# Six plain column blocks instead of four in a ConvGLU mixer, and a later rank for the sums of squares of its norm

## The chip, the core and the metric

The kernel runs on one NeuronCore of a Trainium2 chip. The metric is the device time of one execution in microseconds; before and after are compared by the median of several runs. The engines are named as the profile names them: PE (TensorE matmul), PEld (its weight loads), DVE (VectorE), ACT (ScalarE), POOL (GpSimd), SP (SyncE, which issues the DMAs here).

## What is computed

An encoder trunk of two layers over 512 positions of width 1024, all in float32. Cut to what matters here:

```python
for l in range(DEPTH):                                   # DEPTH = 2
    ...                                                  # attention: two head groups, then
    x = x + jnp.einsum('bsm,md->bsd', y, w_out[l])       # the output projection
    h = rmsnorm(x, g_ffn[l])                             # x * rsqrt(mean(x*x) + EPS) * g
    gate, val = jnp.split(jnp.einsum('bsd,df->bsf', h, w_up[l]), 2, axis=-1)
    gate = centred_dwconv(gate, conv_w[l], conv_b[l])    # width 3
    x = x + jnp.einsum('bsf,fd->bsd', jax.nn.silu(gate) * val, w_down[l])
```

D_FF is 2816: 22 blocks f of 128 columns, each with a gate product and a value product of depth 1024.

## The kernel before

**Layout and products.** The residual stream x lies in SBUF as eight tiles x_0 to x_7 of 128 features by 512 positions. A float32 product is made of three fast ones: each operand is split into a rounded high part and the rest (h and l; wh and wl for weights), and a product is high by high, high by low, low by high, all summed in one PSUM bank (`mm3`). A weight unit is loaded by SP into `wr`, rounded by ACT (a CAST to `wh`), and the rest is taken by DVE (`wl<-wr,wh`). There are two `wr` buffers and three each of `wh` and `wl`.

**The norm of the mixer (class `Norm`, name nf).** The mixer's products run on g*x without the factor r = rsqrt(mean square); r is applied later. `add(k)` makes nf_h (ACT) and nf_l (DVE) of tile k as soon as the last output projection has added to x_k. `squares` makes x_k*x_k on ACT (`nf_q`, the first straight into `nf_sum`) and adds it into `nf_sum` on DVE. `rms` then takes the sum over features with eight PE records (`nf_ss`), DVE makes `nf_v`, POOL `nf_r` by a power, and `rb_track` spreads r over the partitions with PE (`rps`) and copies it on ACT (`rb`).

**The plain path (`up_step`).** One product of 24 matmuls of 512 columns for the gate of block f (`up_f_0`), one for its value (`up_f_1`). The gate's bank is freed when DVE has made `gp = bank * rb`; then come the conv (`cv`, ACT and two DVE instructions), SiLU (ACT), `cv * rb` on POOL, the multiplication by the value's bank on DVE, and the split for the down projection (`act_out`). Five PSUM banks serve these products.

**The halved pairs (`pair_step`, `up_pair`).** Two blocks f and f+1 together as a 2 by 2 block product with seven half products instead of eight: 84 matmuls of 256 columns for the gates, 84 for the values. They need "forms" of h (sums and differences of halves, `ha` to `fc`, made once per layer by `mixer_forms` as soon as rb is there), four sums of weights on DVE per pair and half (`ws`), and DVE puts the results together (`du`, `gp`, `dp`). The last half product of a pair must wait for the first `du`.

**Order.** `mixer_order` gives, for the first part (blocks 0 to 5), four plain blocks and the pair 4; after that pairs 6, 8, 10, ... stand between the steps of the down projection `dn`. `PLAIN` is the number of plain blocks. The order of every engine is fixed when the program is built: a planner (`Machine.run`, line 258 is its issuing line, so all trace rows carry L258) takes the operation that can start first, and among those that can start within a short hold the one with the smallest rank. The ranks stand in `RK`: `xl` 8 for the last additions to x and the nf_h and nf_l after them, `w` 2, 45 or 30 for weight units (36 `wf` when one is ready ahead in the mixer), `hf` 22 for the forms, `nsq` for the squares and their sums. Engines then run their queues in that order; a waiting instruction holds everything behind it on its engine.

Of the kernel before, what the change touches and what calls it, by code (L numbers as in the profile page):

```python
# [26 lines left out]
EPS = 1e-6  # L27
NEG = -1e30
FF_PARTS = ((0, 6), (6, 12), (12, 18), (18, 22))
PLAIN = 4  # L30
CHUNKS = ("akv", "aq0", "aq1", "bv0", "bk1", "bk0", "bq0", "bq1", "bv1")
CW = 256
RP = 4
# [11 lines left out]


RK = {"w": (2, 45, 30), "qkb": (55, 18), "x": 33, "xl": 8, "a": 2, "b": 18, "evac": 49, "qka": 60, "kv": 45,
      "bn": 2, "nsq": 6, "av": -4, "bv": 4, "ch": 50, "add": 42, "sec": 1, "nxs": 42, "fin": 42, "sum": 25,
      "hf": 22, "wf": 36}


# [250 lines left out]
def kernel(  # L302
# [72 lines left out]
    def mixer_order():  # L375

        ups = [[(f, 1) for f in range(f0, min(f1, PLAIN))] + [(f, 2) for f in range(max(f0, PLAIN), f1, 2)]
               for f0, f1 in FF_PARTS]
        for f, n in ups[0]:
            yield "up", 0, f, n  # L380
        for pi in range(len(FF_PARTS)):
            after = ups[pi + 1] if pi + 1 < len(FF_PARTS) else []
            at = {NK * i // len(after): u for i, u in enumerate(after)}
            for d in range(NK):
                if d in at:
                    yield ("up", pi + 1, *at[d])
                yield "dn", pi, d, 0
# [277 lines left out]
    def layer(l, norm):  # L665
# [862 lines left out]
        def ffn():  # L1528
            steps = list(mixer_order())
            b_st["rb_left"] = PLAIN + 1  # L1530
            mix["forms"] = 14
# [149 lines left out]
```

## Time and profile before

| | |
|---|---|
| median of 3 runs | 1184.47 us (1183.8 to 1187.16) |
| the profiled execution: time, span | 1185.19 us, 1183.1 us |
| busy in the span: PE, DVE, ACT, POOL | 98%, 83%, 56%, 17% |
| mean granted TensorE clock | 0.993 |
| first mixer product of layer 0, of layer 1 | starts 236.20 us, 823.03 us |
| first halved pair of layer 0, of layer 1 | starts 288.48 us, 875.38 us |

The span runs from the first to the last instruction of the core. Matmuls are pipelined, so a row's duration (0.39 us for 512 columns) is longer than the step to the next row's start (0.2275 us): what a matmul costs in a stream is read from starts, and where PE is late is seen where the step between two starts is longer than that. Where a row has a pair of brackets, the engine stood idle for that time before it, and the name behind the arrow ended it.

### The profile page before, as it was taken

Reading aid. Unit: us, or ns where it says so; the run is one execution under the profiler, and the core shown is the slowest. Engines: PE = TensorE matmul, PEld = TensorE weight load, DVE = VectorE, ACT = ScalarE, POOL = GpSimd, SP = SyncE. Lnnn points to the kernel's source line nnn. Section 1 sums busy time; section 2 is a strip of 40 time slices with the busy share of each in tenths; the row PEclk is TensorE's granted clock in tenths of the full one; section 3 lists DMA queues with packets and bytes.
Section 4 is the critical chain, followed back from the end, with each engine's and each line's share of the span. In section 5 each row is a group of like instructions: output and inputs, shape, how many; then the busy total and the mean of one; then the engine's idle time right before and its main releaser. Section 6 shows DMA issues by size and latency. Waiting matters only on the chain.

```text
span 1183.1 us, 20177 instructions
## 1 busy us (share of the span) xinstructions
PE 1163.1 (98%) x7796; PEld 1053.0 (89%) x7796; DVE 981.9 (83%) x1797; ACT 663.2 (56%) x1187; POOL 202.3 (17%) x254
## 2 busy tenths in 40 slices
PE   9999999999999999999999989999999999999998
PEld 7999888978999999999889989888789999999997
DVE  6988899779998888887659888898799988888863
ACT  6779766455564454444537876665555544544441
POOL 2433721010100000000042556110111000000000
PEclk9999999989999999999999999999899999999999
DMA  6221111123223322332332121111232223233323
GB/s 233 66 72 55 54 55 36 54 72 107 68 99 112 111 99 99 112 125 71 107 118 73 37 71 37 55 54 54 71 124 61 96 88 112 98 112 103 121 81 116
DMA packets 33343, 103.12 MB, mean 87 GB/s; under 512 B 3936, under 2 KB 4192, under 8 KB 33248
## 3 DMA queue, kind: packets, MB, share of 16 engines
q1 hardware_dynamic: 33248, 101.84, 26.0%
q8 instruction: 61, 1.00, 0.4%
q14 instruction: 34, 0.28, 0.1%
HBM read 99.73 MB, written 2.10 MB: 86 GB/s over the span
## 4 chain that ended last, share of the span: by engine, by line
PE 79%; DVE 13%; ACT 5%; issue 2%; POOL 0%; DMA 0%; SPq 0%; DVEq 0%; ACTq 0%
PE up L258 32%; PE dn L258 20%; PE wo L258 6%; PE pj_bk L258 3%; PE pj_bv L258 2%; PE pj_akq L258 2%; PE pj_bq L258 2%; DVE wl L258 2%; PE yb L258 2%; PE sc_b L258 2%; PE pt_a L258 1%; PE pv_a L258 1%; PE sc_a L258 1%; PE wt_b L258 1%; ACT so_a L258 1%
## 5 line engine op out<-in xcount | busy, mean ns | idle before, releaser
L258 ACT CAST wh<-wr 128x1024 fp32r<-128x1024 f32 (+2 forms) x200 | 177.2, 887 | 158.9 <-PE up L258 41.3
L258 DVE TENSOR_TENSOR wl<-wr,wh 128x1024 fp32r<-128x1024 f32 (+2 forms) x193 | 196.7, 1020 | 62.9 <-ACT wh L258 62.7
L258 ACT CAST wh<-ws 128x1024 fp32r<-128x1024 f32 x72 | 75.4, 1048 | 109.2 <-DVE ws L258 46.1
L258 PE MATMUL up<-fc,wh 128*128 128x256 f32 x576 | 106.4, 285 | 1.8 <-DVE du L258 1.8
L258 PE MATMUL up<-fa,wh 128*128 128x256 f32 x576 | 107.0, 283 | 0.0
L258 PE MATMUL up<-fb,wh 128*128 128x256 f32 x576 | 105.6, 284 | 0.0
L258 PEld LDWEIGHTS up<-fc,wh 128*128 128x128 f32 x576 | 89.4, 191 | 2.6 <-ACT cv L258 2.1
L258 PEld LDWEIGHTS up<-fb,wh 128*128 128x128 f32 x576 | 89.8, 192 | 0.4 <-ACT dp L258 0.2
L258 PEld LDWEIGHTS up<-fa,wh 128*128 128x128 f32 x576 | 89.8, 192 | 0.1
L258 DVE TENSOR_TENSOR wl<-ws,wh 128x1024 fp32r<-128x1024 f32 x72 | 89.5, 1245 | 0.4 <-ACT wh L258 0.2
L258 PE MATMUL dn<-act,wh 128*128 128x512 f32 x288 | 88.9, 390 | 0.0
L258 PE MATMUL up<-fa,wl 128*128 128x256 f32 x288 | 81.7, 284 | 0.0
L258 PE MATMUL up<-fb,wl 128*128 128x256 f32 x288 | 81.5, 283 | 0.0
L258 PE MATMUL up<-fc,wl 128*128 128x256 f32 x288 | 81.4, 283 | 0.0
L258 PE MATMUL dn<-acth,wh 128*128 128x512 f32 x208 | 81.0, 389 | 0.0
L258 PE MATMUL dn<-actl,wh 128*128 128x512 f32 x208 | 81.0, 389 | 0.0
L258 PE MATMUL dn<-acth,wl 128*128 128x512 f32 x208 | 80.9, 389 | 0.0
L258 POOL TENSOR_TENSOR du<-du 128x256 f32<-128x256 f32 x12 | 8.9, 742 | 395.9 <-DVE du L258 395.9
L258 DVE TENSOR_TENSOR x<-x,dn 128x512 f32<-128x512 f32 x64 | 43.7, 682 | 32.8 <-PE dn L258 32.8
L258 DVE SCALAR_TENSOR_TENSOR cv<-gp,cols,cv 128x512 f32<-128x512 f32 x88 | 63.9, 745 | 0.0
L258 PEld LDWEIGHTS dn<-act,wh 128*128 128x128 f32 x288 | 53.3, 188 | 10.4
L258 ACT ACTIVATE e_b<-sc_b,mx_b,rqb 128x512 f32<-128x512 f32 x64 | 49.1, 776 | 14.6 <-DVE mx_b L258 14.6
(269 smaller groups left out, 3452.4 us busy)
## 6 DMA issues: line engine op xcount, KB each, us to landing
wr<-w_up SPq DMA_DIRECT2D x88, 512.0 KB, 4.5
wr<-w_down SPq DMA_DIRECT2D x48, 384.0 KB, 3.1
wr<-w_in SPq DMA_DIRECT2D x28, 512.0 KB, 3.5
wr<-w_out SPq DMA_DIRECT2D x16, 512.0 KB, 3.4
wr<-w_down SPq DMA_DIRECT2D x16, 256.0 KB, 2.6
x<-xT SPq DMA_DIRECT2D x8, 256.0 KB, 5.5
prob_f<-w_first SPq DMA_DIRECT2D x8, 256.0 KB, 5.6
wr<-w_first SPq DMA_DIRECT2D x4, 512.0 KB, 3.6
```

Of the source, the lines that this page charges most:

```text
L258: getattr(self.raw[op.eng], op.name)(*op.args, **op.kw)
```

## The change

Two numbers. `PLAIN` goes from 4 to 6: in each layer blocks 4 and 5 are made by two plain steps instead of one halved pair, so the whole first part is plain and the pair 6 is the first. And the rank `nsq` goes from 6 to 44: the squares of the mixer's norm and their sums give way to everything with a smaller rank, among it the nf_h and nf_l (8) and weight units that are needed (2).

```diff
-PLAIN = 4
+PLAIN = 6
...
-      "bn": 2, "nsq": 6, "av": -4, "bv": 4, "ch": 50, "add": 42, "sec": 1, "nxs": 42, "fin": 42, "sum": 25,
+      "bn": 2, "nsq": 44, "av": -4, "bv": 4, "ch": 50, "add": 42, "sec": 1, "nxs": 42, "fin": 42, "sum": 25,
```

The planner makes new orders of it. DVE's queue in layer 0 where the output projection ends and the mixer begins, before (x are the last additions, nf_l the low parts that PE waits for, nf_sum the sums of squares, wl weight units):

```order
L258 TENSOR_TENSOR x_71<-x_71,wo_2_1_5_3062 128x256
L258 SCALAR_TENSOR_TENSOR nf_l_3082<-x_68,cols,nf_h_3064 128x512
L258 TENSOR_TENSOR wl_3068<-wr_2873,wh_3052 128x1024
L258 SCALAR_TENSOR_TENSOR nf_l_3094<-x_69,cols,nf_h_3078 128x512
L258 TENSOR_TENSOR nf_sum<-nf_sum,nf_q_3098 128x512
L258 SCALAR_TENSOR_TENSOR nf_l_3119<-x_70,cols,nf_h_3085 128x512
L258 TENSOR_TENSOR nf_sum<-nf_sum,nf_q_3121 128x512
L258 SCALAR_TENSOR_TENSOR nf_l_3128<-x_71,cols,nf_h_3091 128x512
L258 TENSOR_TENSOR nf_sum<-nf_sum,nf_q_3130 128x512
L258 TENSOR_TENSOR x_72<-x_72,wo_2_1_6_3074 128x256
L258 TENSOR_TENSOR nf_sum<-nf_sum,nf_q_3137 128x512
L258 TENSOR_TENSOR x_73<-x_73,wo_2_1_7_3087 128x256
```

The same place after:

```order
L258 TENSOR_TENSOR x_71<-x_71,wo_2_1_5_3063 128x256
L258 TENSOR_TENSOR wl_3060<-wr_2873,wh_3052 128x1024
L258 SCALAR_TENSOR_TENSOR nf_l_3076<-x_68,cols,nf_h_3065 128x512
L258 SCALAR_TENSOR_TENSOR nf_l_3087<-x_69,cols,nf_h_3070 128x512
L258 SCALAR_TENSOR_TENSOR nf_l_3097<-x_70,cols,nf_h_3078 128x512
L258 SCALAR_TENSOR_TENSOR nf_l_3107<-x_71,cols,nf_h_3082 128x512
L258 TENSOR_TENSOR x_72<-x_72,wo_2_1_6_3074 128x256
L258 TENSOR_TENSOR x_73<-x_73,wo_2_1_7_3091 128x256
L258 TENSOR_TENSOR wl_3114<-wr_2957,wh_3101 128x1024
L258 SCALAR_TENSOR_TENSOR nf_l_3132<-x_72,cols,nf_h_3128 128x512
L258 SCALAR_TENSOR_TENSOR nf_l_3139<-x_73,cols,nf_h_3130 128x512
L258 TENSOR_TENSOR nf_sum<-nf_sum,nf_q_3055 128x512
```

All seven additions into nf_sum now stand behind the last nf_l; one more weight unit (wl_3114) has come ahead of the last two nf_l. Layer 1 has the same order.

PE's queue at the same place, before (nf_ss is the sum over features, rps the spreading of r):

```order
L258 MATMUL up_0_0_3100<-nf_h_3148,wl_2942 128x512
L258 MATMUL nf_ss<-unit,nf_sum 128x1 x4
L258 MATMUL up_0_1_3166<-nf_h_3023,wh_3052 128x512
L258 MATMUL up_0_1_3166<-nf_l_3030,wh_3052 128x512
L258 MATMUL up_0_1_3166<-nf_h_3023,wl_3068 128x512
```

And after:

```order
L258 MATMUL up_0_1_3152<-nf_h_3130,wl_3060 128x512
L258 MATMUL nf_ss<-unit,nf_sum 128x1 x4
L258 MATMUL up_1_0_3200<-nf_h_3023,wh_3101 128x512
L258 MATMUL up_1_0_3200<-nf_l_3030,wh_3101 128x512
L258 MATMUL up_1_0_3200<-nf_h_3023,wl_3114 128x512
```

nf_ss has moved from behind the first product to behind the second; rps follows nine matmuls after nf_ss in both.

DVE's queue at the first `du` of the first halved pair of layer 0, before (pair 4; actl is the low part of a finished block, wl units are weights of this pair):

```order
L258 TENSOR_TENSOR wl_3598<-wr_1_3345,wh_3592 128x512
L258 TENSOR_TENSOR actl_1_3572<-cv_1_3280,acth_1_3571 128x512
L258 SCALAR_TENSOR_TENSOR cv_2_3386<-gp_2_3385,cols,cv_2_3386 128x512
L258 TENSOR_TENSOR wl_3618<-wr_0_3349,wh_3611 128x1024
L258 TENSOR_TENSOR du_4_0_3529<-dp_4_0_3528,up_4_0_3_3610 128x256
```

And after (pair 6):

```order
L258 TENSOR_TENSOR actl_4_3736<-cv_4_3566,acth_4_3735 128x512
L258 SCALAR_TENSOR_TENSOR cv_5_3650<-gp_5_3649,cols,cv_5_3650 128x512
L258 TENSOR_TENSOR wl_3758<-wr_1_3524,wh_3752 128x512
L258 TENSOR_TENSOR du_6_0_3692<-dp_6_0_3691,up_6_0_3_3771 128x256
L258 TENSOR_TENSOR wl_3778<-wr_0_3531,wh_3772 128x1024
```

The 1024-wide weight unit that stood ahead of the first du now stands behind it. Apart from blocks 4 and 5 and the places of nf_ss and rps, PE's order of products is the same in both programs, in both layers.

## Rows read from the trace of the kernel before

**Rows 1.** The page: busy time of the engines with share of the span, and the chain of work that ended last, by engine.

```profile
PE 1163.1 (98%) x7796; PEld 1053.0 (89%) x7796; DVE 981.9 (83%) x1797; ACT 663.2 (56%) x1187; POOL 202.3 (17%) x254
...
PE 79%; DVE 13%; ACT 5%; issue 2%; POOL 0%; DMA 0%; SPq 0%; DVEq 0%; ACTq 0%
```

**Rows 2.** Busy time by stretch at the start of the mixer of layer 0 (236 us on) and layer 1 (823 us on). Columns: stretch, its length, busy us and instructions of PE, PEld, DVE, ACT, POOL, then granted clock, DMA share, GB/s.

```profile
236.20:241.30 5.10, 4.49 (x19) 2.90 (x18) 5.10 (x8) 4.62 (x8) 0.00 (x0) 1.00 0.30 103
241.30:244.70 3.40, 1.97 (x6) 0.74 (x5) 3.40 (x7) 2.38 (x4) 0.00 (x0) 1.00 0.00 0
244.70:251.60 6.90, 6.74 (x20) 5.67 (x21) 3.15 (x5) 1.05 (x1) 2.08 (x5) 0.51 0.43 143
...
828.40:831.80 3.40, 1.79 (x6) 0.78 (x6) 3.40 (x8) 2.38 (x4) 0.00 (x0) 1.00 0.00 0
831.80:838.70 6.90, 6.90 (x22) 5.80 (x23) 2.88 (x4) 1.05 (x1) 2.08 (x5) 0.51 0.48 149
```

**Rows 3.** PE in order of time, layer 0, from the first mixer product to the first halved pair (up<-f). Columns: start us, duration us, then the instruction; in brackets the idle time before it and what ended it.

```profile
236.20 0.40 PE L258 MATMUL up<-nf_h,wh 128*128 128x512 f32 x1
...
239.81 0.50 PE L258 MATMUL up<-nf_l,wh 128*128 128x512 f32 x1 [0.30 <-DVE nf_l L258]
...
242.76 0.50 PE L258 MATMUL up<-nf_h,wh 128*128 128x512 f32 x1 [0.95 <-ACT nf_h L258]
...
245.88 1.70 PE L258 MATMUL nf_ss<-unit,nf_sum 128*128 128x1 f32 x8
247.44 0.77 PE L258 MATMUL up<-nf_h,wh 128*128 128x512 f32 x1
...
251.43 1.12 PE L258 MATMUL rps<-ident,nf_r 128*128 128x128 f32 x8
252.31 0.48 PE L258 MATMUL up<-nf_h,wh 128*128 128x512 f32 x1
...
288.48 0.40 PE L258 MATMUL up<-f,wh 128*128 128x256 f32 x2
```

**Rows 4.** The same of layer 1: first mixer product, the longest wait, the first halved pair.

```profile
823.03 0.40 PE L258 MATMUL up<-nf_h,wh 128*128 128x512 f32 x1
...
829.59 0.49 PE L258 MATMUL up<-nf_h,wh 128*128 128x512 f32 x1 [0.95 <-ACT nf_h L258]
...
875.38 0.40 PE L258 MATMUL up<-f,wh 128*128 128x256 f32 x2
```

**Rows 5.** Busy time of PE alone by stretch: 159 plain matmuls of layer 0, its first two pairs, one later pair, the first two pairs of layer 1. Columns: stretch, length, busy us and records, granted clock, DMA share, GB/s.

```profile
252.31:288.48 36.17, 36.17 (x163) 1.00 0.30 103
288.48:330.38 41.90, 41.00 (x337) 1.00 0.23 73
370.99:391.19 20.20, 20.20 (x170) 1.00 0.17 50
875.38:917.27 41.89, 41.01 (x338) 1.00 0.22 68
```

**Rows 6.** DVE in order of time at the start of the mixer of layer 0.

```profile
234.34 0.69 DVE L258 TENSOR_TENSOR nf_sum<-nf_sum,nf_q 128x512 f32<-128x512 f32 x1
234.95 1.08 DVE L258 TENSOR_TENSOR x<-x,wo 128x256 f32<-128x256 f32 x3
235.94 0.75 DVE L258 SCALAR_TENSOR_TENSOR nf_l<-x,cols,nf_h 128x512 fp32r<-128x512 f32 x1
236.60 1.22 DVE L258 TENSOR_TENSOR wl<-wr,wh 128x1024 fp32r<-128x1024 f32 x1
237.74 0.74 DVE L258 SCALAR_TENSOR_TENSOR nf_l<-x,cols,nf_h 128x512 fp32r<-128x512 f32 x1
238.40 0.69 DVE L258 TENSOR_TENSOR nf_sum<-nf_sum,nf_q 128x512 f32<-128x512 f32 x1
239.00 0.75 DVE L258 SCALAR_TENSOR_TENSOR nf_l<-x,cols,nf_h 128x512 fp32r<-128x512 f32 x1
...
244.06 0.74 DVE L258 SCALAR_TENSOR_TENSOR nf_l<-x,cols,nf_h 128x512 fp32r<-128x512 f32 x1
...
247.62 0.16 DVE L258 TENSOR_SCALAR nf_v<-nf_ss 128x4 f32<-128x4 f32 x1 [1.07 <-PE nf_ss L258]
247.70 1.23 DVE L258 TENSOR_TENSOR wl<-wr,wh 128x1024 fp32r<-128x1024 f32 x1
```

**Rows 7.** ACT in order of time at the same place: a square, the rounding of the next weight unit, a nf_h, the copy rb.

```profile
233.69 0.61 ACT L258 ACTIVATE nf_q<-x 128x512 f32<-128x512 f32 x1
234.21 1.03 ACT L258 CAST wh<-wr 128x1024 fp32r<-128x1024 f32 x1
...
241.98 0.72 ACT L258 ACTIVATE nf_h<-x,cols 128x512 fp32r<-128x512 f32 x1 [1.17 <-DVE x L258]
...
252.65 0.59 ACT L258 COPY rb<-rps 128x512 f32<-128x512 f32 x1 [5.86 <-PE rps L258]
```

**Rows 8.** POOL: the power that makes nf_r in layer 0 (order of time), and, by tile, another power of the same size (count, then shortest, median and longest in ns).

```profile
247.86 1.93 POOL L258 TENSOR_TENSOR nf_r<-nf_v,unit 128x4 f32<-128x4 f32 x1 [26.38 <-DVE nf_v L258]
...
L258 POOL TENSOR_TENSOR rr_yb<-rr_yb,unit x8: 1006/1006/1011, 173.1 to 809.7; 128x4 f32<-128x4 f32 x8
```

**Rows 9.** The first du of layer 0: who waited for whom (PE, whole span: total us, times, longest), and DVE in order of time there.

```profile
PE up L258 <- DVE du L258: 1.8, 2, 0.9
...
295.90 0.74 DVE L258 SCALAR_TENSOR_TENSOR cv<-gp,cols,cv 128x512 f32<-128x512 f32 x1
296.56 1.21 DVE L258 TENSOR_TENSOR wl<-wr,wh 128x1024 fp32r<-128x1024 f32 x1
297.70 0.74 DVE L258 TENSOR_TENSOR du<-dp,up 128x256 f32<-128x256 f32 x2
```

## The prediction

> **What bounds the kernel now.** I read the page first: PE is busy for 98% of the span and carries 79% of the chain that ended last; DVE is at 83% [rows 1]. So two things can save time: fewer or cheaper PE steps, and stretches in which PE stands or runs slowly. The second is sought in a table by stretch. At the start of the mixer, in both layers, the reader is to see PE's busy time fall to 1.97 of 3.40 us and 1.79 of 3.40 us while DVE is busy for all of it, and then a granted clock of 0.51 over 6.90 us, so the 1.2 GHz level, although PE is busy again [rows 2]. In order of time PE waits there for nf_l (DVE) and nf_h (ACT), 0.30 to 0.95 us each [rows 3, 4]. DVE's own rows say why: between one nf_l and the next stands an addition into nf_sum, so nf_l come 1.26 us apart (237.74, 239.00) where PE needs one every three matmuls [rows 6]. The additions have rank 6, the nf_l rank 8.
>
> How much is lost there: from the first mixer product to the first halved pair 52.28 us pass in layer 0 (288.48 - 236.20) and 52.35 us in layer 1 (875.38 - 823.03) [rows 3, 4]. A plain matmul costs 36.17 us / 159 = 0.2275 us at full clock (159 of the 8 x 24 = 192 stand in that stretch) [rows 5]. 192 of them are 43.68 us; rps takes 0.88 us (252.31 - 251.43) and nf_ss, also eight records, is put at the same 0.9. That makes 45.5 us. Lost: **6.8 us in each layer**. Of this the clock is about 3.4 us (6.90 us at half), the waits the rest.
>
> **The late rank (nsq), layer 0.** Everything up to x_68 stands as before, so I walk DVE's new queue from 234.34, with steps read from start to start: nf_sum 0.60, nf_l 0.66, wl 1.14, a half-width x about 0.36 [rows 6]. The nf_sum of 234.34 is gone, but x_71 waits for PE's projection (0.72 us per step up to 236.20, so its step ends at 234.76) and ends at about 235.4. The next wl can follow at once, since its CAST loses the square ahead of it and starts near 233.7 instead of 234.21 [rows 7]: 235.4 to 236.5. Four nf_l end at 237.25, 237.9, 238.6 and 239.2. PE wants them at 236.20 + (3k+1) x 0.2275 for tile k: 237.8, 238.5, 239.2 and 239.8. No wait. Then x_72 and x_73 to 239.9, and here the new order puts a wl of 1.14 us ahead of the nf_l of tile 6: that is readable near 241.8, PE wants it at 240.5. **PE waits 1.3 us**, 1.4 with the slower restart (the wait row of 239.81 shows a 0.50 us record instead of 0.40 behind it). Bounds: 0.7, if the wl ran earlier, to 1.9.
>
> The sums then stand after 242.4, with the squares on ACT behind a CAST that waits for the end of the first product (near 243.1): seven additions and a wl end near 248.1. nf_ss is now behind the second product, near 248.5, so it is covered, by some 0.4 us; when that cover is gone, PE waits for the rest. Behind nf_ss: nf_v 0.18 us later, nf_r 0.24 us after that, 1.93 us long, so 2.35 us from the end of nf_ss (247.44) to nf_r's end (249.79) [rows 3, 6, 8]. Before, nine matmuls at half clock took 3.99 us (247.44 to 251.43) and hid it. Now nine at full clock take 2.05 us, so rps waits 0.3 us, 0.4 with the restart. From below: the same power of 128x4 takes 1.006 us elsewhere [rows 8], with which nothing would be waited for. I keep 0.4, because a wl with two SBUF operands follows nf_v on DVE again, as it does in the row with 1.93.
>
> The Trainium skill (SBUF — State Buffer, section "Who interferes with whom") says that a VectorE instruction with two SBUF inputs and a GpSimd one that reads SBUF exclude each other. The two durations agree with it, and by it the 0.4 us stays.
>
> rb then follows rps at about 252.9, no later than now (252.65) [rows 7], with PE 24 matmuls further on. So the mixer's start keeps 1.8 of the 6.8 us: **5.0 us gained per layer, 10.0 in both** (layer 1 has the same order and nearly the same times [rows 2, 4]). The clock: the five waits become one of 1.3 us and one of 0.3, five microseconds and more apart, with full rows between them, so I take the 2.4 GHz level as kept.
>
> **Six plain blocks.** A pair's 168 matmuls of 256 columns take 20.20 us [rows 5]. Two plain blocks are 4 x 24 matmuls, 96 x 0.2275 = 21.84 us. PE's work grows by 1.64 us per layer: **3.3 us lost**, on the path, with nothing to hide it.
>
> In return the first pairs lose their wait. The first two pairs of a layer take 41.90 and 41.89 us, 1.5 us more than 2 x 20.20 [rows 5]; most of it is the first du, 0.89 to 0.9 us late, because DVE, in arrears, began a 1024-wide wl at 296.56 just ahead of it [rows 9]. After the change the forms are made beside eight more plain products of 5.46 us, four of them in place of the pair, and only a 512-wide wl stands ahead of the first du. From rb to the first ws of pair 6 DVE's queue holds 63 instructions: 7 wl of 1.14, 15 of 0.66, 21 of 0.60 and 20 half-width ones of 0.36, 37.7 us in all; it is there near 291 us, PE at the pair near 305. I take 1.3 us per layer as returned: **2.6 us gained**, bounds 0 and 3.0. Of what else is removed on DVE and ACT (sums of weights, CASTs of weight sums) nothing counts, as it lies beside PE. The added cv * rb on POOL (17% busy) lie beside it too. The same bytes of w_up are loaded.
>
> New waits could come from the five banks: the sixth plain product, near 267, needs the first bank back, which gp frees near 256.6, 10 us earlier. Blocks 4 and 5 write their split into buffers that nf_h and nf_l free only after the last plain product, near 305; the first dn needs them a whole pair, 20 us, later.
>
> **Sum.** -10.0 + 3.3 - 2.6 = -9.3 us against the profiled execution's own 1185.19 us: 1175.9. That execution lies 0.7 us above the median of the runs shown (1184.47): **1175.1 us**.
>
> **Rivals.**
> (a) *The clock falls all the same.* PE still waits once in the first product, then runs eight small nf_ss and a short wait. If this is enough, 3.4 us per layer come back: 1178.5 for one layer, 1181.9 for both. For: the level fell although no wait was longer than 0.95 us [rows 3]. Against: then five waits followed each other within 6 us, now one stands alone.
> [...]
> (b) *Nothing is kept.* nf_l and nf_r come in time and the du waits vanish: -13.6 - 3.0 + 3.3 = -13.3, so 1171.2. For: 1.006 us for the same power [rows 8]. Against: the wl ahead of the nf_l of tile 6 is in the queue.
> (c) *Slower: the sums come too late.* They now run in one block with only 0.4 us of cover ahead of nf_ss, on DVE between weight units and on ACT behind a CAST that waits for PE. [...] Against: the walk gives 248.1, and a single weight unit more is 1.14 us.
> (d) *The planner's change does not bind*, as PE was never the loser at these places: then only the 3.3 us of work are left, 1187.8. Against: the wait rows [rows 3, 9].
>
> **Chances.** Forecast (1173 to 1178) 0.62; (a) 0.15, two thirds of it with one layer; (b) 0.15; (c) 0.05; (d) 0.03. What a measurement of this kernel can tell from no change is about 0.3%, 3.6 us, so faster means below 1180.9: forecast, (b) and one-layer (a) give 0.87; same: two-layer (a) and a mild (c), 0.08; slower 0.05. The range takes in (b) and one-layer (a) with the run-to-run spread: 1171 to 1180.
>
> **What would show it.** In the profile after: a granted clock of 1.00 through the start of both mixers; one PE wait of about 1.3 us for the nf_l of tile 6 in the first product and about 0.3 us before rps; pair 6 starting near 305.4 us after 65.5 + 1.8 + 1.8 us of plain products; no PE wait for du; pairs and dn otherwise as now; span near 1173.8. Wrong it would be if PE waited at nf_ss, if the clock row showed 0.5 there, or if PE waited in the plain products 6 to 12 for banks or weights.

## The result and the profile after

The changed kernel takes 1174.99 us (median of 4 runs, 1174.19 to 1176.04) against 1184.13 us (1182.13 to 1187.16) for the kernel before on the same chip: ratio 0.9922, 95% interval 0.9903 to 0.9942. Faster by 9.1 us, where 9.3 were predicted. The profiled execution took 1176.04 us, its span 1174.3 us.

The page, busy time and chain, against [rows 1]:

```profile
PE 1157.8 (99%) x7652; PEld 1043.2 (89%) x7652; DVE 967.8 (82%) x1753; ACT 653.5 (56%) x1169; POOL 202.2 (17%) x258
...
PE 76%; DVE 11%; issue 6%; ACT 4%; DMA 1%; POOL 1%; SPq 0%; ACTq 0%; POOLq 0%; DVEq 0%
```

Busy time by stretch at the start of both mixers (columns as in [rows 2]): first product up to the wait, the rest of two products, then nf_ss, nine matmuls and rps.

```profile
236.97:242.00 5.03, 4.61 (x21) 3.38 (x19) 5.03 (x9) 4.15 (x7) 0.00 (x0) 1.00 0.32 104
242.00:249.44 7.44, 6.89 (x30) 5.33 (x30) 6.86 (x10) 4.07 (x8) 0.00 (x0) 1.00 0.45 141
249.44:253.63 4.19, 4.11 (x24) 3.38 (x25) 1.30 (x2) 0.80 (x1) 2.08 (x5) 1.00 0.20 36
...
819.03:824.06 5.03, 4.61 (x21) 3.38 (x19) 5.03 (x9) 4.15 (x7) 0.00 (x0) 1.00 0.35 104
824.06:831.50 7.44, 6.92 (x30) 5.34 (x30) 6.86 (x10) 4.04 (x8) 0.00 (x0) 1.00 0.44 139
```

The granted clock is 1.00 in all these stretches, so the 2.4 GHz level; in [rows 2] it was 0.51 over 6.90 us in each layer. (The profile as a whole has a mean of 0.998: 3.41 us at half lie in the attention of layer 1, as they do in the profile of the kernel before.)

PE in order of time (columns as in [rows 3]), both layers:

```profile
236.97 0.40 PE L258 MATMUL up<-nf_h,wh 128*128 128x512 f32 x1
...
242.45 0.50 PE L258 MATMUL up<-nf_l,wh 128*128 128x512 f32 x1 [0.87 <-DVE nf_l L258]
...
248.95 0.39 PE L258 MATMUL up<-nf_h,wl 128*128 128x512 f32 x1
249.44 1.05 PE L258 MATMUL nf_ss<-unit,nf_sum 128*128 128x1 f32 x8
...
252.28 0.39 PE L258 MATMUL up<-nf_h,wl 128*128 128x512 f32 x1
252.75 1.16 PE L258 MATMUL rps<-ident,nf_r 128*128 128x128 f32 x8
...
306.12 0.40 PE L258 MATMUL up<-f,wh 128*128 128x256 f32 x2
...
819.03 0.40 PE L258 MATMUL up<-nf_h,wh 128*128 128x512 f32 x1
824.51 0.50 PE L258 MATMUL up<-nf_l,wh 128*128 128x512 f32 x1 [0.88 <-DVE nf_l L258]
...
888.18 0.40 PE L258 MATMUL up<-f,wh 128*128 128x256 f32 x2
```

One bracket per layer is left of the five in the kernel before, two of which [rows 3] show. From the first product to the first pair 69.15 us pass in both layers (306.12 - 236.97, 888.18 - 819.03). Without loss it would be 288 x 0.2275 + 1.8 = 67.3, so 1.83 us are lost per layer, where 6.8 were before. Two losses too short for a bracket show in the steps between starts: nf_ss comes 0.49 us after its forerunner and rps 0.47, where a matmul takes 0.2275, so 0.26 and 0.24 us late.

DVE and POOL there (as [rows 6, 8]):

```profile
239.85 0.75 DVE L258 TENSOR_TENSOR x<-x,wo 128x256 f32<-128x256 f32 x2
240.51 1.22 DVE L258 TENSOR_TENSOR wl<-wr,wh 128x1024 fp32r<-128x1024 f32 x1
241.65 1.41 DVE L258 SCALAR_TENSOR_TENSOR nf_l<-x,cols,nf_h 128x512 fp32r<-128x512 f32 x2
...
246.31 3.07 DVE L258 TENSOR_TENSOR nf_sum<-nf_sum,nf_q 128x512 f32<-128x512 f32 x4
250.53 0.16 DVE L258 TENSOR_SCALAR nf_v<-nf_ss 128x4 f32<-128x4 f32 x1 [1.15 <-PE nf_ss L258]
250.60 1.23 DVE L258 TENSOR_TENSOR wl<-wr,wh 128x1024 fp32r<-128x1024 f32 x1
```

```profile
250.77 1.93 POOL L258 TENSOR_TENSOR nf_r<-nf_v,unit 128x4 f32<-128x4 f32 x1 [28.51 <-DVE nf_v L258]
```

The wl of 1.22 us stands ahead of the nf_l of tile 6 as the order said; the last nf_sum ends at 249.38, 0.2 us after PE wants nf_ss (249.18).

Among PE's waits the du of [rows 9] is gone, and the mixers have one kind left:

```profile
PE up L258 <- DVE nf_l L258: 1.7, 2, 0.9
```

Where the 8.8 us of span went (a mixer is counted from the start of PE's first product in it to that of the first attention product behind it, in layer 1 to that of PE's last matmul): the mixer of layer 0 takes 350.92 us instead of 355.44, that of layer 1 350.77 instead of 355.99, so 9.74 us less; the first mixer begins 0.77 us later, the attention of layer 1 is 0.25 shorter, and the tail behind PE's last matmul is 0.4 longer.

### The profile page after: what moved, and what is told of

Its sections match the earlier page's. It is cut to its first block, busy times and chain, and to the rows that moved or that the text cites. A ratio compares the mean times of both kernels' runs of the same rounds, so it can differ in the third digit from the quotient of the medians.

```text
span 1174.3 us, 19830 instructions
## 1 busy us (share of the span) xinstructions
PE 1157.8 (99%) x7652; PEld 1043.2 (89%) x7652; DVE 967.8 (82%) x1753; ACT 653.5 (56%) x1169; POOL 202.2 (17%) x258
## 4 chain that ended last, share of the span: by engine, by line
PE 76%; DVE 11%; issue 6%; ACT 4%; DMA 1%; POOL 1%; SPq 0%; ACTq 0%; POOLq 0%; DVEq 0%
PE up L258 30%; PE dn L258 20%; PE wo L258 5%; PE pj_bk L258 3%; PE pj_akq L258 3%; PE pj_bv L258 2%; PE pj_bq L258 2%; PE yb L258 2%; DVE wl L258 2%; PE sc_b L258 2%; PE pt_a L258 1%; PE pv_a L258 1%; PE sc_a L258 1%; PE wt_b L258 1%; DVE cv L258 1%
## 5 line engine op out<-in xcount | busy, mean ns | idle before, releaser
L258 ACT CAST wh<-ws 128x1024 fp32r<-128x1024 f32 x64 | 66.9, 1048 | 101.6 <-DVE ws L258 37.7
L258 PE MATMUL up<-fa,wh 128*128 128x256 f32 x512 | 94.9, 283 | 0.0
L258 PE MATMUL up<-fc,wh 128*128 128x256 f32 x512 | 94.2, 284 | 0.0
L258 PE MATMUL up<-fb,wh 128*128 128x256 f32 x512 | 93.7, 283 | 0.1
L258 PEld LDWEIGHTS up<-fb,wh 128*128 128x128 f32 x512 | 79.8, 192 | 0.5 <-ACT dp L258 0.5
L258 PEld LDWEIGHTS up<-fa,wh 128*128 128x128 f32 x512 | 79.9, 192 | 0.0
L258 PEld LDWEIGHTS up<-fc,wh 128*128 128x128 f32 x512 | 79.6, 191 | 0.0
L258 DVE TENSOR_TENSOR wl<-ws,wh 128x1024 fp32r<-128x1024 f32 x64 | 78.9, 1235 | 0.0
L258 PE MATMUL up<-nf_l,wh 128*128 128x512 f32 x192 | 75.0, 391 | 1.7 <-DVE nf_l L258 1.7
L258 PE MATMUL up<-nf_h,wh 128*128 128x512 f32 x192 | 75.3, 392 | 0.0
L258 PE MATMUL up<-nf_h,wl 128*128 128x512 f32 x192 | 74.8, 389 | 0.0
```

Source lines behind the costliest of these rows:

```text
L258: getattr(self.raw[op.eng], op.name)(*op.args, **op.kw)
```

## The experiments

All are edits of these two kernels. Medians, with the kernel before of the same chip at 1184.57 (first four), 1184.91 (next four) and 1185.12 us (last two):

| kernel | median us | ratio to before (95%) | first product to first pair, layer 0 / 1 |
|---|---|---|---|
| plain half alone | 1185.42 | 1.0014 (1.0 to 1.0029) | 74.86 / 73.52 |
| rank half alone | 1192.49 | 1.0079 (1.0052 to 1.0105) | 47.39 / 47.75 |
| changed, hold in both layers | 1177.16 | 0.9948 (0.9930 to 0.9966) | 67.92 / 67.91 |
| changed, two holds | 1177.73 | 0.9950 (0.9934 to 0.9965) | 67.92 / 67.96 |
| rank half, light DVE | 1189.74 | 1.0046 (1.0029 to 1.0063) | 47.45 / 47.43 |
| rank half, two plain blocks | 1223.32 | 1.0334 (1.0310 to 1.0359) | 25.07 / 25.05 |
| changed, heavy DVE | 1179.58 | 0.9965 (0.9951 to 0.9979) | 70.75 / 70.72 |
| changed, hold in layer 1 | 1175.32 | 0.9926 (0.9898 to 0.9954) | 69.17 / 67.91 |
| changed, rank 9 | 1175.02 | 0.9916 (0.9899 to 0.9934) | 68.92 / 68.91 |
| changed, light DVE | 1180.52 | 0.9963 (0.9949 to 0.9976) | 69.15 / 69.17 |

### The two halves apart

```diff
-PLAIN = 4
+PLAIN = 6
```

> Six plain blocks with the old rank 6 of the sums of squares: the work half of the change alone. DVE's and PE's order at the mixer's start is that of the kernel before. Theory (terms of the prediction add up): the five waits and the stretch of about 6.8 us at the 1.2 GHz level stay in both layers (0 of the 10.0 us gained), the added work costs 3.3 us, the first pairs' wait for du goes (-2.6): +0.7 us, so about 1184.8 us, first mixer product to first pair 52.3 + 21.84 = 74.1 us per layer. Rival: what clears the mixer's start is not the rank but the plain blocks (later forms, other weight units ahead): then the clock stays at 1.00 and the time is near 1175.

Measured: 1185.42 us; the forecast was 1184.8, and the interval (1.0 to 1.0029) reaches from no loss to 3.4 us. Busy time by stretch at the mixers' start (columns as in [rows 2]), then PE's waits (whole span: total, times, longest):

```profile
246.30:253.30 7.00, 7.00 (x25) 6.13 (x26) 1.67 (x3) 0.62 (x1) 2.08 (x5) 0.50 0.47 150
...
836.40:842.40 6.00, 6.00 (x26) 5.25 (x26) 1.61 (x3) 0.67 (x2) 2.08 (x5) 0.65 0.55 173
```

```profile
PE up L258 <- ACT nf_h L258: 1.9, 2, 1.0
PE up L258 <- DVE nf_l L258: 1.9, 6, 0.3
PE up L258 <- DVE du L258: 0.4, 2, 0.2
```

The clock falls again in both layers (10.24 us at half in layer 0, where the kernel before had 6.83, and 6.83 in layer 1), and PE waits for nf_h and nf_l nearly as before. So the plain blocks don't clear the mixer's start; the next kernel shows that the rank does. The du wait shrinks from 1.8 to 0.4 us in all.

```diff
-"nsq": 6
+"nsq": 44          (with PLAIN = 4)
```

> Four plain blocks with the new rank 44: the rank half alone. The mixer's start has the order of the changed kernel, pair 4 is the first pair again. Theory A (terms independent): the mixer's start gains 5.0 us per layer and nothing else moves: about 1174.3 us, with the first pair starting 47.3 us after the first mixer product and its wait for du 0.9 us as before. Theory B (DVE's queue between rb and the first du sets when the first pair can go on): rb comes no earlier than before while PE comes to the pair 5 us sooner, so that PE waits some 5 us more in the first pair of each layer, and most of the gain is eaten: 1180 to 1184 us. By B the two halves of the change need one another.

Measured: 1192.49 us, **slower than before by 7.9 us**, beyond theory B. The start gains what was forecast (47.39 and 47.75 us to the first pair, where 52.28 and 52.35 were before; the clock is 1.00), and the first pairs lose it all and more. PE in order of time in the first pair and at the second, layer 0, then DVE there:

```profile
284.87 0.40 PE L258 MATMUL up<-f,wh 128*128 128x256 f32 x2
287.29 0.38 PE L258 MATMUL up<-f,wh 128*128 128x256 f32 x1 [1.18 <-ACT f L258]
288.12 0.39 PE L258 MATMUL up<-f,wh 128*128 128x256 f32 x1 [0.45 <-DVE f L258]
290.53 0.39 PE L258 MATMUL up<-fa,wh 128*128 128x256 f32 x1 [0.70 <-DVE fa L258]
292.73 0.50 PE L258 MATMUL up<-fb,wh 128*128 128x256 f32 x2 [1.69 <-ACT dp L258]
...
315.86 0.47 PE L258 MATMUL up<-fa,wh 128*128 128x256 f32 x2 [2.44 <-DVE dp L258]
```

```profile
285.25 0.75 DVE L258 SCALAR_TENSOR_TENSOR ha<-x,cols,rb 128x512 f32<-128x512 f32 x1
285.91 0.75 DVE L258 SCALAR_TENSOR_TENSOR hb<-x,cols,rb 128x512 f32<-128x512 f32 x1
...
287.27 0.80 DVE L258 TENSOR_TENSOR f<-ha,f 128x256 fp32r<-128x256 f32 x1
```

Busy time by stretch ahead of the pair (columns as in [rows 2]):

```profile
270.00:284.87 14.87, 14.87 (x67) 12.30 (x66) 14.87 (x25) 6.63 (x10) 0.54 (x3) 1.00 0.23 73
```

The reader is to see that DVE is busy for all of 14.87 us and only at 285.25 begins the last set of forms, when PE has been at the pair since 284.87. From the first to the second pair 26.71 us pass and to the third 31.33, where 20.20 and 28.39 are what a pair and a pair with its down step take in later rows: 9.4 us lost. In the kernel before the same two distances were 21.37 and 28.73, so 1.5 us lost, as [rows 5] gave for two pairs. So 7.9 us go per layer against the 4.9 and 4.6 that the start gains. Theory B named the place and was too low: it counted the 5 us by which PE comes sooner. The brackets shown sum to 6.5 us, and behind them the clock falls (3.41 us at half in each layer, from 293.60 and from 884.10, about 1.7 us of work); how much of the rest is slow restarts the rows don't part.

### Less and more work for DVE

```diff
-            yield dve.scalar_tensor_tensor(out=cv, in0=g[:, 0:S], ...)
-            yield dve.scalar_tensor_tensor(out=cv, in0=g[:, 2:S + 2], ...)
+            if f >= 4:
+                (the same two)
```

> As the rank half alone (four plain blocks, rank 44; 1192.5 us), but the convolution of blocks 0 to 3 leaves out its two DVE instructions (the outer two of three taps): eight instructions of 0.66 us less on DVE per layer, 5.3 us, seven or eight of them between rb and the first pair; nothing is taken from PE. Theory (DVE's queue between rb and the forms of the first pair is the bound there): PE's waits for f, fa and dp in the first pair shrink by 4.5 to 5.3 us in each layer, and a clock fall may go with them: 1180 to 1184 us. Rival (the forms are late by their place in the order or by ACT's roundings, not by the amount of DVE work): the waits stay, 1191 to 1193 us.

Measured: 1189.74 us, faster than the rank half by 2.7 us and not by the 8 to 12 expected. The waits for f and fa are gone, so the amount of DVE work was what made the forms late; but one wait of 4.6 us per layer stands in their place (PE's waits, whole span: total, times, longest; then PE and DVE in order of time, layer 0):

```profile
PE up L258 <- DVE cv L258: 9.2, 2, 4.6
...
289.89 0.79 PE L258 MATMUL up<-fa,wh 128*128 128x256 f32 x2 [4.57 <-DVE cv L258]
...
289.16 0.68 DVE L258 TENSOR_TENSOR cv<-cv,up 128x512 f32<-128x512 f32 x1
```

It is for a PSUM bank: the planner put DVE's product with the last plain value, which frees the bank, at 289.16, behind the lighter queue of forms. The fall of the clock doesn't go either: in layer 0 it begins during that wait (6.83 us at half from 288.19), in layer 1 0.5 us behind it (3.41 us from 882.11). The mixers gain 1.8 and 2.8 us; the attention of layer 1 then got another order from the planner and took 3.8 us longer (234.89 instead of 231.08). The theory holds on the forms, not on the time: something else that stood late in DVE's queue was waited for. Whether the amount of work or the planner's order put it so late, this run doesn't part.

```diff
-PLAIN = 6
+PLAIN = 2          (rank 44)
```

> Rank 44 and two plain blocks, so that the first halved pair comes 21.8 us earlier than with four, against 10.8 us of DVE work that no longer stands ahead of it (4 wl of 1.14, 2 gp, 4 taps, 2 products, 2 splits of 0.60 to 0.66). Theory (DVE's queue is the bound of the first pair): its lateness grows by 11 us per layer and PE's work falls by 1.6, so 1192.5 + 2 x 9.4 = about 1211 us. Rival (the loss with four plain blocks is a fixed start-up of the forms, which any number of plain blocks pays once): PE's saving alone, 1189 us.

Measured: 1223.32 us. The sign is the theory's, the size is larger: the first pair takes 44.27 us instead of 20.20. Stretches of that pair in layer 0 and 1 (columns as in [rows 2]), then PE's waits:

```profile
261.67:305.94 44.27, 24.79 (x169) 22.71 (x168) 40.29 (x70) 23.31 (x37) 4.10 (x9) 0.77 0.13 42
869.32:913.62 44.30, 24.74 (x170) 22.70 (x169) 40.32 (x70) 23.31 (x37) 4.10 (x9) 0.77 0.12 38
```

```profile
PE up L258 <- ACT f L258: 35.1, 6, 6.0
```

DVE is busy for 40.3 of the 44.3 us and PE for 24.8, at a mean clock of 0.77. ACT's rounding is named as the releaser, yet it is busy for only 23.31 us and itself waits for DVE's ha. So the lateness is no fixed start-up: fewer plain blocks make it larger.

```diff
 for t, k in ((at, i), (bt, i + nk)):
+    for _ in range(2):
         yield dve.scalar_tensor_tensor(out=t[:, :S], in0=x_sb[k], ..., in1=rb, ...)
```

> The changed kernel with the two products by r at the head of each set of forms done twice: 8 more DVE instructions of 0.66 us per layer, 5.3 us, right behind rb; the result is the same. Question: how much cover the six plain blocks leave. By the forms alone (the last is made near 290 us, the first pair starts at 306) there are some 16 us of cover, and the time stays at 1175. By the account of the whole queue, six plain blocks leave 8.7 us less lateness than four had plus 2.3: cover of 2 to 3 us, so PE waits 2.5 to 3 us in the first pair of each layer: about 1180 to 1181 us.

Measured: 1179.58 us, 4.6 more than the changed kernel; the mixers take 1.53 and 1.31 us longer. The total is near the second account, but a layer pays only half of its 2.5 to 3 us, and the place is neither's: PE doesn't wait in the pair but ahead of the last plain product, so that the stretch takes 70.75 instead of 69.15 us, for a bank that gp frees (PE, then DVE, in order of time):

```profile
301.84 0.47 PE L258 MATMUL up<-nf_h,wh 128*128 128x512 f32 x1 [1.30 <-DVE gp L258]
```

```profile
299.74 0.69 DVE L258 TENSOR_TENSOR ws<-wr 128x512 f32<-128x512 f32 x1
300.35 0.74 DVE L258 SCALAR_TENSOR_TENSOR cv<-gp,cols,cv 128x512 f32<-128x512 f32 x1
301.01 1.28 DVE L258 TENSOR_TENSOR gp<-up,rb 128x512 f32<-128x512 f32 x2
```

5.3 us of work cost 1.6 us, so six plain blocks leave about 3.7 us of cover (an estimate: it takes each microsecond past the cover to cost one). In the profiled executions, 1177.90 and 1176.04 us, these 2.8 us are partly made up by the attention of layer 1, 0.65 us shorter without a fall of the clock. That the medians differ by 4.6 us and not by 2.8 goes in part with the clock: the four executions of the heavier kernel at a mean clock of 1.000 took 1177.44 to 1179.63 us (the one of the changed kernel at 1.000 took 1174.19), the other six, at 0.995 to 0.999, took 1179.22 to 1183.22.

The changed kernel with the two taps left out in blocks 0 to 5 (`if f >= 6`):

> The changed kernel without the two outer taps of the convolution in blocks 0 to 5, which leaves out twelve DVE instructions of 0.66 us per layer (8 us). Theory (with six plain blocks DVE's queue is in time, with some 3.8 us to spare by the run with 5.3 us more): the plain blocks stay as they are and at most the 0.27 us that the first pair loses come back in each layer: 1174.5 us. Rival (DVE still sets the pace of the plain blocks or the first pairs somewhere that the waits don't show): 1171 or below.

Measured in the mixers: the plain blocks as before (69.15 and 69.17 us), the first pair at its full 20.20 us, each mixer 0.3 us shorter (350.63 and 350.48). So DVE is in time there, and the rival isn't seen in the mixers. The total of 1180.52 us doesn't answer the question: the attention of layer 1 took another order from the planner (PE waits 1.5 us for rr_yb in it), 236.2 us instead of 231.1, and 6.8 us of it at half clock.

### The rest of the loss at the mixer's start

```diff
+HOLDS = {(1, 0): "nf{}7"}
...
+            if i in holds:                 (ahead of the CAST of unit i)
+                yield m.has(holds[i])
```

> The changed kernel, with the rounding (CAST) of the weight unit of product up_1_0 held until nf_h and nf_l of tile 7 exist, so that its wl does not stand ahead of the nf_l of tile 6 on DVE. Theory: the PE wait for that nf_l (0.87 us idle and a total loss of 1.55 us in the first product, in each layer) shrinks to 0 to 0.3 us: about 2.5 us faster than the changed kernel, near 1172.5. Rival: the nf_l of tile 6 is late because x_72 and nf_h of it are late, whatever DVE does before: then the wait stays and the time is 1175 again; or the held CAST now comes late for up_1_0, and a wait of like size stands there.

Measured: the wait for nf_l shrinks from 0.87 to 0.34 us, nf_ss stands three matmuls later and is in time, rps too, and the stretch takes 67.92 us instead of 69.15. The mixers gain 0.9 and 0.5 us (a du wait of 0.4 comes back), but the attention of layer 1, laid out anew, takes 0.9 us more, and the median is 1177.16, not below the changed kernel. The profiled execution (1175.12 us) was the fastest of five, the others took 1177.09 to 1177.88; what those lost, no trace shows.

The same with a second entry, `(2, 0): "{}_rb"`, and with the holds standing ahead of the wl too:

> As the hold of up_1_0, and the rounding and the wl of the unit of up_2_0 held until rb exists, so that DVE has no wl between nf_v and the forms while POOL makes nf_r. Theory (nf_r is slow because a VectorE instruction with two SBUF operands runs beside it): nf_r takes about 1.0 us instead of 1.9, rps waits 0 us instead of 0.3, so another 0.3 to 0.7 us in both layers: about 1172.0. Rival (nf_r is long for another reason): nf_r stays near 1.9 us and the time equals that of the first hold; or the held unit comes late for up_2_0 and PE waits there.

Measured: 1177.73 us. nf_r takes 1.01 us, but it did so with the first hold already, and rps was in time already; the second hold adds nothing, and the attention of layer 1 took 235.1 us.

The first hold with `if l == 1 and (f, j) in HOLDS`:

> The changed kernel with the hold of the weight unit of up_1_0 in layer 1 alone, so that the attention stays as in the changed kernel, and on PE only nf_ss and rps of layer 1 stand elsewhere. Theory: the first pair of layer 1 starts 67.9 us after the first mixer product instead of 69.15 (layer 0 stays at 69.15), nf_r of layer 1 takes 1.0 us and that of layer 0 1.93 us: 1.2 us faster than the changed kernel, near 1173.8. Rival (the slower total of the hold in both layers came out of the mixer, not out of the attention): 1176 to 1177.

Measured: 69.17 us in layer 0, 67.91 in layer 1, as expected. The mixer of layer 1 is 0.9 us shorter; the mixer of layer 0 and the attention of layer 1, in the order of the changed kernel, are 0.2 and 0.7 longer, and the median of 1175.32 can't be told from that of the changed kernel. In one trace, nf_r in layer 0 and 1 on POOL, then DVE in layer 0 and 1:

```profile
250.14 1.93 POOL L259 TENSOR_TENSOR nf_r<-nf_v,unit 128x4 f32<-128x4 f32 x1 [28.51 <-DVE nf_v L259]
...
833.49 1.01 POOL L259 TENSOR_TENSOR nf_r<-nf_v,unit 128x4 f32<-128x4 f32 x1 [26.50 <-DVE nf_v L259]
```

```profile
249.98 1.23 DVE L259 TENSOR_TENSOR wl<-wr,wh 128x1024 fp32r<-128x1024 f32 x1
...
832.11 1.23 DVE L259 TENSOR_TENSOR wl<-wr,wh 128x1024 fp32r<-128x1024 f32 x1 [0.65 <-ACT wh L259]
833.26 0.16 DVE L259 TENSOR_SCALAR nf_v<-nf_ss 128x4 f32<-128x4 f32 x1
```

In layer 0 a wl begins 0.16 us ahead of the power, in layer 1 it ended ahead of nf_v: 1.93 against 1.01 us.

```diff
-"nsq": 44
+"nsq": 9
```

> Six plain blocks and rank 9 for the sums of squares instead of 44: just behind the nf_h and nf_l (8), but ahead of the weight units that aren't needed yet. PE's, POOL's and SP's queues are those of the changed kernel; on DVE one nf_sum stands ahead of the nf_l of tile 2 and one ahead of that of tile 6, where the changed kernel has a wl of twice the length. Theory (only that the sums give way to nf_l matters, so any rank past 8 does it): first mixer product to first pair 68.6 to 69.2 us in both layers, clock 1.00 there, about 1174.5 us. Rival (the sums must be away from the nf_l altogether): the waits in the first product and the fall of the clock come back, and the time is 1179 to 1182.

Measured: 1175.02 us, the same as with 44; 68.92 us to the first pair, clock 1.00. Two short waits per layer (0.3 us for nf_h, 0.3 for nf_l) stand in the place of the one of 0.87 (PE's waits, whole span):

```profile
PE up L258 <- DVE nf_l L258: 0.7, 2, 0.3
PE up L258 <- ACT nf_h L258: 0.5, 2, 0.3
```

So what matters is that the sums give way to the nf_h and nf_l; between rank 9 and 44, how late they come makes no difference.

## Why the prediction was right

**The mixer's start: right in its size, and partly by luck.** Forecast 1.8 us kept of 6.8, measured 1.83 in both layers, so the 10.0 us forecast for both were gained. The nf_l of tile 6 is the one wait, at 0.87 us plus a slow restart, 1.25 in all, a little under the 1.4 forecast. nf_r was 1.93 us long, and rps 0.24 late, where 0.4 was forecast. The 0.4 us of cover ahead of nf_ss weren't there: the walk had the last nf_sum done at 248.1 and PE there at 248.5; measured were 249.38 and 249.18 (the mixer itself began 0.77 us later than in the walk), and PE waited 0.26. That is rival (c)'s place at its mildest. So three small errors cancelled: 1.25 instead of 1.4, 0.26 instead of nothing, 0.24 instead of 0.4.

**The clock, rival (a): no.** One wait of 0.87 us leaves the 2.4 GHz level standing at the mixer's start in the profiles of all kernels with the late sums that have it; with the five waits the fall is back in the plain half. The Trainium skill (TensorE: Matmul & The Clock Gate, section "A second HAM failure mode: psum-queue depth-cycling") says that frequent short idle times make the clock swing; these runs agree, though here what PE waits for is DVE and ACT. The Trainium skill's section "Why this matters for your kernels" on the same page warns only of long idle gaps between bursts of matmuls; here the fall came without one and went with the short waits. The fall doesn't come in full in every execution, and how much of the gain hangs on it shows in the spread of the kernel before: of the 17 executions beside the first group one had a mean clock of 0.999 and took 1179.56 us, those at 0.993 took 1183.85 to 1185.84. So about half of the 9.1 us is gained even where the clock hardly falls, as far as one execution tells.

**The port.** That nf_r is long because a VectorE instruction with two SBUF operands runs beside it was kept in the sum on the strength of two durations. The two layers of one kernel now show it, 1.93 us with and 1.01 without, as the Trainium skill (SBUF — State Buffer, section "Who interferes with whom") has it.

**The plain blocks: +3.3 - 2.6 = +0.7 forecast for the half alone, +0.9 measured.** The agreement is closer than the measurement, whose interval is 0 to 3.4 us: in the profile the mixer of layer 0 took 2.0 us more than before, with a longer stretch at half clock, and that of layer 1 0.8 less. In the changed kernel the first pairs lose 0.27 us per layer instead of 1.5, so 1.24 came back of the 1.3 forecast; a loss of 0.66 us at the third pair of layer 1 (33.13 instead of 32.47) went too, unforeseen.

**What the sum hid: here the mechanism was wrong, and the number right by luck.** The prediction added three terms as if each stood for itself. The halves alone give +0.9 and +7.9 us, together -9.1: they differ from a sum by 18 us. The step at fault is that of the first pairs: it priced two more plain blocks as the return of a 1.5 us wait (2.6 us, "bounds 0 and 3.0"). In truth they also cover what the earlier start would have made late, 7.9 us per layer in the rank half: rb comes no earlier, as the prediction itself said, but PE stands 5 us further on, and DVE's queue from rb to the first pair was full (in the rank half it was busy for 29.41 of 30.42 us there). The changed kernel's sum came out right because both edits were in it. Its cover was overstated as well. From rb to the first ws of pair 6 DVE took 40.3 us (253.94 to 294.23) where 37.7 were counted. That would still be 11.9 us ahead of the pair, yet an added 5.3 us already cost 1.6, at gp and a bank ahead of the twelfth plain product; the prediction had reckoned the banks for the sixth alone, with 10 us of room there.

**Rivals (b) and (d)** fell: the wl ahead of tile 6 held, and the planner's order did bind.

Left open is the planner's other order of the attention of layer 1, which came with five of the experiments and made it 0.9 to 5 us longer; it lies outside the change. The profiles part it from the clock in part: without a fall there it took 229.61 and 230.49 us in the usual order (rank 9, heavy DVE) and 232.03 in the other (first hold), so about 2 us go with the order. The other four had 3.41 or 6.83 us at half clock and took 234.89 to 236.22, which is more than the half clock alone would add.

## What to carry to other kernels

When a wait at the head of a stage goes, ask where the engine that caused it stands at the stage's next need: here PE gained 5 us on DVE, DVE had none to give, and only the two plain blocks (1.64 us of extra PE work per layer) made room for it. Test the halves of a change apart before crediting a gain to either. In a stage with a full queue on a second engine, price the cover by the whole queue and the last instruction in it, not by the one result that PE seems to wait for.

## What was not expected of the hardware

- A clock fall can outlast the waits ahead of it: in layer 0 of the plain half the last of the waits ended at 243.72, and the clock stood at half from 243.25 to 253.49 though PE shows no idle time behind that wait. With two plain blocks it stood at half for 20.48 us in each layer (from 266.75 and 874.32); there the waits went on, in layer 0 until 283.48.
- The longest wait alone doesn't tell whether the clock falls: one of 1.30 us (heavier DVE) and one of 0.87 us (the changed kernel) left it at 1.00 in their profiles, one of 4.57 us (the rank half with light DVE) had a fall with it, and so had five of 0.3 to 0.95 us close together (0.51 behind them, though not in every execution of the kernel before).
